# A hybrid encoder layer on one core: the end of the output projection, with halves split and part of the LayerNorm on TensorE

## The chip, the cores and the metric

The kernel runs on one core of one Trainium2 chip. The metric is the device time of one execution in microseconds (us). Each kernel also has one profiled execution, whose trace gives the start and length of every instruction; its time is counted from the trace's first to its last instruction (the span) and has a little around it.

The engines are named as in the profile: PE (TensorE, matrix products; PEld is its loading of weights), DVE (VectorE), ACT (ScalarE), POOL (GpSimd), SP (SyncE, which issues the DMAs here). "Granted clock" is the share of TensorE's full clock that the chip allowed at a moment.

## The reference

One layer works on 256 frames of width 4096. One input projection feeds sixteen heads of forgetting attention, 32 heads of an RWKV-7 recurrence and a gate. Their gated outputs `h` go through one output projection, and a LayerNorm closes the layer. What matters here is that end:

```python
h = jnp.concatenate([fox_out, rwkv_out], axis=-1) * jax.nn.silu(z.astype(f32))
out = jnp.einsum('bsc,cd->bsd', h.astype(x.dtype), w_out)
x = _layernorm(ALPHA * x.astype(f32) + out.astype(f32), ln_gain, ln_bias, LN_EPS)
```

where `_layernorm(x)` is `(x - mean) * rsqrt(var + eps) * gain + bias`, with mean and variance over the 4096 columns of a frame.

## The kernel before, in words

The 256 frames are two halves of 128 partitions, m = 0 and 1. The output projection runs over eight column blocks `b` of 512. In each block sixteen weight tiles `wo{b}_{q}` of 128 x 1024 come in from HBM (L651) and are split by `split` into a rounded high part on ACT (L135) and the rest on DVE (L136); each holds two k-slices of 128 rows. The pools behind the high and the low parts hold three tiles each. For each k-slice and each half there are three 512-column products (L663 to L665: high frames x high weights, low x high, high x low), which add up over 32 k-slices in one PSUM bank per half, `acc[m]`. The loop over m is the innermost, so both halves of a block end together.

After a block DVE forms ALPHA x + out in `res[m]` (L678) and its statistics (L679), and in all blocks but the last multiplies by the gain (L682). The residual, the gain and a five-row table `rows` of gain and bias were loaded and made block by block earlier (`load_tok`).

Behind the last block come the row factors, for both halves in one set of small instructions. They are: the statistics put together (L691), the square root on ACT (L692), the reciprocal `rs` (L694), minus mean times `rs` (L695) in a rounded and a rest part (L696 to L698, into `z5`), with the last block's gain products (L693, L699) between them. PE transposes `z5` into `zp` (L703), and ACT copies that into `l5` (L705), a 5 x 128 weight per half.

Then sixteen blocks are finished, half 0 first: a five-row product `l5` x `rows` into a PSUM tile `wp` (L711), and on DVE `res * rs + wp` (L712). Each pair of blocks is sent out by one DMA of 512 KB (L717); the last two blocks of half 1 go one by one (L714).

PSUM has eight banks in two pools. `pp` has two and `ps` six; a new tile of a pool waits until the tile that held its bank is done with. Within an engine instructions run in the order of the program's stream, which the framework's scheduler lays out when the program is built. A DMA waits in SP's queue in order.

Of the kernel before, what the change touches and what calls it, by code (L numbers as in the profile page):

```python
# [10 lines left out]
F32 = mybir.dt.float32  # L11
BF16 = mybir.dt.bfloat16
F32R = mybir.dt.float32r
AF = mybir.ActivationFunctionType
ALU = mybir.AluOpType
AX = mybir.AxisListType

P = 128
S = 256
D = 4096  # L20
KT = D // P
# [6 lines left out]
ALPHA = 2.0 ** 0.25  # L28
# [5 lines left out]
OB = 512  # L34
# [2 lines left out]
ROWS = 2  # L37
W = {"fr": 10, "fo": 3, "vs": 2, "np": 6, "gp": 5, "d1": 8, "d2": 8, "xp": 3, "fs": 4, "fp": 5}
NB = D // OB

PAR = ["w0", "a0", "k_k", "k_a", "r_k", "gn_gain", "gn_bias", "mu_r", "mu_k", "mu_v"]

# [35 lines left out]
def layer(ctx: ExitStack, tc: tile.TileContext, xt, xtok, w_lora, w_main, w_o, up, par, mulora, fbias, lng, lnb, cst, out, groups=G, dbg=None):  # L78
    nc = tc.nc
# [6 lines left out]
    pp = ctx.enter_context(tc.tile_pool(name="pp", bufs=2, space=PS))  # L86
    ps = ctx.enter_context(tc.tile_pool(name="ps", bufs=6, space=PS))
    def pst(name):
        return ps.tile([P, 512], F32, tag="ps", name=name)
# [35 lines left out]
    ident = cs[:, C_ID : C_ID + P]  # L125
# [6 lines left out]
    def split(src, n, name):  # L132
        hi = wpool.tile([P, 1024], F32R, tag="wh", name=name + "h")
        lo = wpool.tile([P, 1024], F32R, tag="wl", name=name + "l")
        nc.scalar.copy(hi[:, :n], src[:, :n])  # L135
        nc.vector.tensor_tensor(lo[:, :n], src[:, :n], hi[:, :n].bitcast(F32), ALU.subtract)  # L136
        return hi, lo
# [8 lines left out]
    for n, (k0, k1) in enumerate(pieces):  # L146
# [6 lines left out]
        hi, lo = split(l_raw[n], (k1 - k0) * LW, f"wl{n}")  # L153
        for k in range(k0, k1):
            o = (k - k0) * LW
            mm(acc_l[0], LORA + NF, hi, lo, o, k)
            mm(acc_l[1], LORA, hi, lo, o + LORA + NF, k)
        hi, lo = split(w_raw[n], (k1 - k0) * P, f"wr{n}")
# [35 lines left out]
    def slot():  # L194
        for g in list(sides):
            try:
                next(g)
            except StopIteration:
                sides.remove(g)
# [415 lines left out]
    ht = {}  # L615

    def get_h(k):
        while k not in hs:
            slot()
        t = xpool.tile([P, 2, S], F32R, tag=f"x{k}", name=f"h{k}")  # L620
        nc.scalar.copy(t[:, 0, :], hs[k])
        nc.vector.tensor_tensor(t[:, 1, :], hs[k], t[:, 0, :].bitcast(F32), ALU.subtract)
        ht[k] = t
# [6 lines left out]
    def load_tok(b):  # L630
        o = slice(b * OB, (b + 1) * OB)
        for m in range(2):
            nc.sync.dma_start(out=res[m][:, o], in_=xtok[m * P : (m + 1) * P, o])
        nc.sync.dma_start(out=lgain[:, o], in_=lng[:, o].to_broadcast([P, OB]))
        rr = rpool.tile([5, OB], F32, tag="rr", name=f"rr{b}")
        nc.sync.dma_start(out=rr[0:3], in_=lng[:, o].to_broadcast([3, OB]))
        nc.sync.dma_start(out=rr[3:5], in_=lnb[:, o].to_broadcast([2, OB]))
        rh = rpool.tile([5, OB], F32R, tag="rh", name=f"rh{b}")
        nc.scalar.copy(rh, rr)
        rt_ = rpool.tile([5, OB], F32, tag="rt", name=f"rt{b}")  # L640
        nc.vector.tensor_scalar(rt_, rh.bitcast(F32), cs[0:5, C_ROW : C_ROW + 1], None, ALU.mult)
        nc.vector.scalar_tensor_tensor(rows[:, o], rr, cs[0:5, C_ROW + 1 : C_ROW + 2], rt_, ALU.mult, ALU.add)

    res = None
    st = [const.tile([P, NB, 6], F32, name=f"lst{m}") for m in range(2)]
    for b in range(NB):
        pool, tag = (pp, "pp") if b % 2 == 0 else (ps, "ps")
        acc = [pool.tile([P, 512], F32, tag=tag, name=f"oacc{b}_{m}") for m in range(2)]
        for q in range(KT // 2):
            raw = wpool.tile([P, 1024], F32, tag="wr", name=f"wo{b}_{q}", bufs=4)  # L650
            nc.sync.dma_start(out=raw, in_=w_o[b][:, 2 * q : 2 * q + 2, :].rearrange("p k c -> p (k c)"))  # L651
            hi, lo = split(raw, 1024, f"wo{b}_{q}")
            for j in range(2):
                k = 2 * q + j
                if b == 0:
                    slot()
                    get_h(k)
                elif k == 4:
                    load_tok(b)
                o = slice(j * OB, (j + 1) * OB)  # L660
                for m in range(2):
                    tt = slice(m * P, (m + 1) * P)
                    nc.tensor.matmul(acc[m], ht[k][:, 0, tt], hi[:, o], start=(k == 0), stop=False)  # L663
                    nc.tensor.matmul(acc[m], ht[k][:, 1, tt], hi[:, o], start=False, stop=False)  # L664
                    nc.tensor.matmul(acc[m], ht[k][:, 0, tt], lo[:, o], start=False, stop=(k == KT - 1))  # L665
        if b == 0:
            assert not sides
            mid.close()
            rpool = ctx.enter_context(tc.tile_pool(name="rpool", bufs=1))
            res = [rpool.tile([P, D], F32, tag=f"res{m}", name=f"res{m}") for m in range(2)]  # L670
            lgain = rpool.tile([P, D], F32, name="lgain")
            rows = rpool.tile([5, D], F32R, name="rows")
            load_tok(0)
            lneps = const.tile([P, 1], F32, name="lneps")
            nc.vector.memset(lneps, LN_EPS)
        for m in range(2):
            o = slice(b * OB, (b + 1) * OB)
            nc.vector.scalar_tensor_tensor(res[m][:, o], res[m][:, o], ALPHA, acc[m], ALU.mult, ALU.add)  # L678
            nc.vector.bn_stats(st[m][:, b, :], res[m][:, o])  # L679
        if b < NB - 1:  # L680
            for m in range(2):
                nc.vector.tensor_tensor(res[m][:, o], res[m][:, o], lgain[:, o], ALU.mult)  # L682
    o = slice(D - OB, D)
    mv = rpool.tile([P, 2, 2], F32, name="mv")
    rs = rpool.tile([P, 2], F32, name="rs")
    s2 = rpool.tile([P, 2], F32, name="s2")
    zh = rpool.tile([P, 2], F32R, name="zh")
    z5 = rpool.tile([P, 2, 5], F32, name="z5")
    nc.vector.memset(z5, 1.0)
    for m in range(2):  # L690
        nc.vector.bn_aggr(mv[:, m, :], st[m].rearrange("p b s -> p (b s)"))  # L691
    nc.scalar.activation(rs, mv[:, :, 1], AF.Sqrt, bias=lneps)  # L692
    nc.vector.tensor_tensor(res[0][:, o], res[0][:, o], lgain[:, o], ALU.mult)  # L693
    nc.vector.reciprocal(rs, rs)  # L694
    nc.vector.scalar_tensor_tensor(s2, mv[:, :, 0], -1.0, rs, ALU.mult, ALU.mult)  # L695
    nc.vector.tensor_copy(zh, s2)  # L696
    nc.vector.tensor_copy(z5[:, :, 0:3:2], zh.bitcast(F32).unsqueeze(2).to_broadcast([P, 2, 2]))
    nc.vector.tensor_tensor(z5[:, :, 1], s2, zh.bitcast(F32), ALU.subtract)  # L698
    nc.vector.tensor_tensor(res[1][:, o], res[1][:, o], lgain[:, o], ALU.mult)  # L699
    l5 = []  # L700
    for m in range(2):
        zp = pst(f"zp{m}")
        nc.tensor.transpose(zp[:5, :P], z5[:, m, :], ident)  # L703
        t = rpool.tile([5, P], F32R, name=f"l5{m}")
        nc.scalar.copy(t, zp[:5, :P])  # L705
        l5.append(t)
    for m in range(2):
        for b in range(NB):
            o = slice(b * OB, (b + 1) * OB)
            wp = pp.tile([P, 512], F32, tag="pp", name=f"wp{m}_{b}") if b % 2 else pst(f"wp{m}_{b}")  # L710
            nc.tensor.matmul(wp, l5[m], rows[:, o], start=True, stop=True)  # L711
            nc.vector.scalar_tensor_tensor(res[m][:, o], res[m][:, o], rs[:, m : m + 1], wp, ALU.mult, ALU.add)  # L712
            if m == 1 and b >= NB - 2:
                nc.sync.dma_start(out=out[m * P : (m + 1) * P, o], in_=res[m][:, o])  # L714
            elif b % 2:
                o = slice((b - 1) * OB, (b + 1) * OB)
                nc.sync.dma_start(out=out[m * P : (m + 1) * P, o], in_=res[m][:, o])  # L717


def arrange(inputs):  # L720
# [10 lines left out]
    res["w_main"] = np.ascontiguousarray(np.stack([t.reshape(KT, P, G, P).transpose(2, 1, 0, 3) for t in (r, k, v, fq, fk, fv, zf, zr)], 1))  # L731
    wo = a["w_out"].reshape(2, G, P, NB, OB)
    res["w_o"] = np.ascontiguousarray(wo.transpose(3, 2, 1, 0, 4).reshape(NB, P, KT, OB))
# [27 lines left out]
```

## Time and profile before

| | |
|---|---|
| median of 3 runs | 2077.0 us (2075.1 to 2077.57) |
| profiled execution | 2079.26 us |
| its span | 2077.5 us |
| mean granted TensorE clock over the span | 0.993 |
| output written by the last nine DMAs | 4.19 MB |

Times in the rows below are microseconds from the span's start. A row of the timeline gives start, length, engine, line, operation, result<-operands, and how many instructions were merged into it, then the idle time before it and who ended it. A row of a table by stretches gives the stretch, its length, the busy time of each engine with its instructions (xN), then the granted clock, the share of the DMA engines in use and GB/s.

### The profile page before, as it was taken

Reading aid. Unit: us, or ns where it says so; the run is one execution under the profiler, and the core shown is the slowest. Engines: PE = TensorE matmul, PEld = TensorE weight load, DVE = VectorE, ACT = ScalarE, POOL = GpSimd, SP = SyncE. Lnnn points to the kernel's source line nnn. Section 1 sums busy time; section 2 is a strip of 40 time slices with the busy share of each in tenths; the row PEclk is TensorE's granted clock in tenths of the full one; section 3 lists DMA queues with packets and bytes.
Section 4 is the critical chain, followed back from the end, with each engine's and each line's share of the span. In section 5 each row is a group of like instructions: output and inputs, shape, how many; then the busy total and the mean of one; then the engine's idle time right before and its main releaser. Section 6 shows DMA issues by size and latency. Waiting matters only on the chain.

```text
span 2077.5 us, 32862 instructions
## 1 busy us (share of the span) xinstructions
PE 2030.4 (98%) x12430; PEld 1711.2 (82%) x12430; DVE 1482.1 (71%) x2919; ACT 1017.7 (49%) x1607; POOL 25.0 (1%) x138
## 2 busy tenths in 40 slices
PE   9999999999999999999999999999999999999997
PEld 7878888888888888888888888888887878888885
DVE  6867777777777767677777777777776786655555
ACT  6635454545454545454545454545453564433331
POOL 0000000000000000000000000000000000000000
PEclk9999999999999999999999999999999999999998
DMA  7545555555555555555555555555555557866664
GB/s 275 181 159 165 179 166 179 166 179 166 179 167 178 170 174 172 173 166 179 166 179 166 178 167 176 168 178 164 178 165 161 171 165 237 261 192 193 192 194 150
DMA packets 130862, 372.71 MB, mean 179 GB/s; under 512 B 31160, under 2 KB 40040, under 8 KB 130704
## 3 DMA queue, kind: packets, MB, share of 16 engines
q1 hardware_dynamic: 130704, 370.62, 56.0%
q8 instruction: 97, 1.59, 0.3%
q14 instruction: 61, 0.50, 0.1%
HBM read 364.23 MB, written 6.32 MB: 178 GB/s over the span
## 4 chain that ended last, share of the span: by engine, by line
PE 71%; DVE 17%; DMA 8%; issue 2%; SPq 1%; ACT 1%; DVEq 0%; ACTq 0%
PE acc L140 31%; PE acc L141 15%; PE oacc L663 6%; PE oacc L664 6%; PE oacc L665 6%; DVE xc L456 4%; DVE prod L455 3%; DVE w_1l L136 3%; DMA td<-xc 2%; DMA Nb<-nd 2%; DMA T<-td 2%; DMA nd<-gb 2%; DVE w_2l L136 2%; DVE w_3l L136 1%; DVE w_0l L136 1%
## 5 line engine op out<-in xcount | busy, mean ns | idle before, releaser
L140 PE MATMUL acc<-x,w_1h 128*128 128x512 f32 x1016 | 372.7, 403 | 0.4 <-ACT w_1h L135 0.4
L140 PE MATMUL acc<-x,w_2h 128*128 128x512 f32 x1016 | 372.6, 404 | 0.0
L140 PE MATMUL acc<-x,w_3h 128*128 128x512 f32 x1016 | 369.1, 401 | 0.0
L140 PE MATMUL acc<-x,w_0h 128*128 128x512 f32 x1016 | 369.1, 401 | 0.0
L141 PE MATMUL acc<-x,w_1l 128*128 128x256 f32 x1016 | 289.2, 285 | 23.5 <-DVE w_1l L136 23.5
L141 PE MATMUL acc<-x,w_2l 128*128 128x256 f32 x1016 | 284.9, 280 | 0.0
L141 PE MATMUL acc<-x,w_0l 128*128 128x256 f32 x1016 | 284.6, 280 | 0.0
L141 PE MATMUL acc<-x,w_3l 128*128 128x256 f32 x1016 | 284.3, 280 | 0.0
L140 PEld LDWEIGHTS acc<-x,w_1h 128*128 128x128 f32 x1016 | 191.7, 189 | 44.1 <-ACT w_1h L135 1.2
L140 PEld LDWEIGHTS acc<-x,w_0h 128*128 128x128 f32 x1016 | 190.6, 188 | 45.3
L140 PEld LDWEIGHTS acc<-x,w_3h 128*128 128x128 f32 x1016 | 190.5, 188 | 44.9
L140 PEld LDWEIGHTS acc<-x,w_2h 128*128 128x128 f32 x1016 | 191.5, 189 | 41.3
L141 PEld LDWEIGHTS acc<-x,w_1l 128*128 128x128 f32 x1016 | 192.9, 190 | 33.6 <-DVE w_1l L136 33.6
L135 ACT CAST w_2h<-w 128x1024 fp32r<-128x1024 f32 x127 | 133.2, 1049 | 133.7 <-PE acc L140 119.2
L135 ACT CAST w_0h<-w 128x1024 fp32r<-128x1024 f32 x127 | 133.2, 1049 | 126.6 <-PE acc L140 92.4
L141 PEld LDWEIGHTS acc<-x,w_2l 128*128 128x128 f32 x1016 | 192.3, 189 | 0.9 <-DVE w_2l L136 0.2
L141 PEld LDWEIGHTS acc<-x,w_3l 128*128 128x128 f32 x1016 | 191.8, 189 | 1.0 <-DVE w_3l L136 0.3
L141 PEld LDWEIGHTS acc<-x,w_0l 128*128 128x128 f32 x1016 | 191.9, 189 | 0.5 <-DVE w_0l L136 0.3
L136 DVE TENSOR_TENSOR w_0l<-w,w_0h 128x1024 fp32r<-128x1024 f32 x127 | 155.3, 1223 | 51.4 <-ACT w_0h L135 51.4
L135 ACT CAST w_1h<-w 128x1024 fp32r<-128x1024 f32 x127 | 132.8, 1046 | 105.2 <-PE acc L140 77.2
L136 DVE TENSOR_TENSOR w_2l<-w,w_2h 128x1024 fp32r<-128x1024 f32 x127 | 155.1, 1221 | 34.2 <-ACT w_2h L135 32.6
L136 DVE TENSOR_TENSOR w_1l<-w,w_1h 128x1024 fp32r<-128x1024 f32 x127 | 154.4, 1216 | 31.2 <-ACT w_1h L135 28.3
(691 smaller groups left out, 3228.5 us busy)
## 6 DMA issues: line engine op xcount, KB each, us to landing
w<-in_w_main_dram SPq DMA_DIRECT2D x508, 512.0 KB, 4.5
wo<-in_w_o_dram SPq DMA_DIRECT2D x128, 512.0 KB, 3.5
Nb<-nd SPq DMA_DIRECT2D x16, 512.0 KB, 5.0
res<-in_xtok_dram SPq DMA_DIRECT2D x16, 256.0 KB, 4.8
xr<-in_xt_dram SPq DMA_DIRECT2D x7, 512.0 KB
out_dram<-res SPq DMA_DIRECT2D x7, 512.0 KB, 2.7
lr<-in_w_lora_dram SPq DMA_DIRECT2D x7, 416.0 KB, 8.4
nb<-ncd SPq DMA_DIRECT2D x16, 128.0 KB, 4.7
```

The source lines that it names most:

```text
L135: nc.scalar.copy(hi[:, :n], src[:, :n])
L136: nc.vector.tensor_tensor(lo[:, :n], src[:, :n], hi[:, :n].bitcast(F32), ALU.subtract)
L140: nc.tensor.matmul(acc[:m, :], hi[:, o : o + m], xs[k].rearrange("p a t -> p (a t)"), start=(k == 0), stop=False)
L141: nc.tensor.matmul(acc[:m, :S], lo[:, o : o + m], xs[k][:, 0, :], start=False, stop=(k == KT - 1))
L455: nc.vector.tensor_tensor(prod[:, :, s + 1 :], nb[:, s : s + 1, s + 1 :].to_broadcast([P, NJ, w]), xc[:, :, s + 1 :], ALU.mult)
L456: nc.vector.tensor_reduce(xc[:, :, s : s + 1], prod[:, :, s:], AX.X, ALU.add)
L663: nc.tensor.matmul(acc[m], ht[k][:, 0, tt], hi[:, o], start=(k == 0), stop=False)
L664: nc.tensor.matmul(acc[m], ht[k][:, 1, tt], hi[:, o], start=False, stop=False)
L665: nc.tensor.matmul(acc[m], ht[k][:, 0, tt], lo[:, o], start=False, stop=(k == KT - 1))
```

## The change

The last three weight tiles (q = 13, 14, 15) of the last block are used half by half: half 1's eighteen products over them are put off until half 0's are all issued (`late`). The row factors are computed for each half by itself (`moments`, `row`), so that half 0's stand in the program ahead of half 1's end. The tile of ones under `z5` is set on POOL and no longer on DVE.

In three of the eight blocks of each half (1, 4 and 6) the finishing is done by PE and ACT: PE multiplies `res` by a 128 x 128 diagonal matrix `dg` of the row factors in 32-bit floating point, adds the five-row product into the same bank, and ACT copies the sum to `res`. The other five blocks are finished by DVE as before. `pp` holds the tiles of blocks 3 and 7, `ps` all others. `send` issues the same nine DMAs.

```diff
+LATE = 3
+BY_PE = (1, 4, 6)
...
                 for m in range(2):
-                    tt = slice(m * P, (m + 1) * P)
-                    nc.tensor.matmul(acc[m], ht[k][:, 0, tt], hi[:, o], start=(k == 0), stop=False)
-                    nc.tensor.matmul(acc[m], ht[k][:, 1, tt], hi[:, o], start=False, stop=False)
-                    nc.tensor.matmul(acc[m], ht[k][:, 0, tt], lo[:, o], start=False, stop=(k == KT - 1))
+                    if m and b == NB - 1 and q >= KT // 2 - LATE:
+                        late.append((k, j, hi, lo))
+                    else:
+                        project(acc[m], k, j, m, hi, lo)
...
+    def moments(m):
+        nc.vector.scalar_tensor_tensor(res[m][:, o], res[m][:, o], ALPHA, acc[m], ALU.mult, ALU.add)
+        nc.vector.bn_stats(st[m][:, NB - 1, :], res[m][:, o])
...
+        nc.gpsimd.memset(z5, 1.0)
+        nc.vector.bn_aggr(mv, st[m].rearrange("p b s -> p (b s)"))
+        nc.scalar.activation(rs, mv[:, 1:2], AF.Sqrt, bias=lneps)
+        nc.vector.tensor_tensor(res[m][:, o], res[m][:, o], lgain[:, o], ALU.mult)
+        nc.vector.reciprocal(rs, rs)
+        nc.vector.scalar_tensor_tensor(s2, mv[:, 0:1], -1.0, rs, ALU.mult, ALU.mult)
+        nc.vector.tensor_copy(zh, s2)
+        d = rpool.tile([P, P], F32, name=f"dg{m}")
+        nc.scalar.mul(d, ident, rs)
+        nc.vector.tensor_copy(z5[:, 0:3:2], zh.bitcast(F32).to_broadcast([P, 2]))
+        nc.vector.tensor_tensor(z5[:, 1:2], s2, zh.bitcast(F32), ALU.subtract)
...
+    def row(m, z5):
+        zp = pst(f"zp{m}")
+        nc.tensor.transpose(zp[:5, :P], z5, ident)
+        t = rpool.tile([5, P], F32R, name=f"l5{m}")
+        nc.scalar.copy(t, zp[:5, :P])
+        l5.append(t)
+
+    def finish(m, b):
+        o = slice(b * OB, (b + 1) * OB)
+        wp = pp.tile([P, 512], F32, tag="pp", name=f"wp{m}_{b}") if b % 4 == 3 else pst(f"wp{m}_{b}")
+        if b in BY_PE:
+            nc.tensor.matmul(wp, dg[m], res[m][:, o], start=True, stop=False)
+            nc.tensor.matmul(wp, l5[m], rows[:, o], start=False, stop=True)
+            nc.scalar.copy(res[m][:, o], wp)
+        else:
+            nc.tensor.matmul(wp, l5[m], rows[:, o], start=True, stop=True)
+            nc.vector.scalar_tensor_tensor(res[m][:, o], res[m][:, o], rss[m], wp, ALU.mult, ALU.add)
...
+    z0 = moments(0)
+    for k, j, hi, lo in late:
+        project(acc[1], k, j, 1, hi, lo)
+    row(0, z0)
+    finish(0, 0)
+    finish(0, 1)
+    z1 = moments(1)
+    send(0, 0, 2)
+    for b in range(2, NB):
+        if b == 4:
+            row(1, z1)
+        finish(0, b)
+        if b % 2:
+            send(0, b - 1, b + 1)
+    for b in range(NB):
+        finish(1, b)
+        if b >= NB - 2:
+            send(1, b, b + 1)
+        elif b % 2:
+            send(1, b - 1, b + 1)
```

In the built program PE's stream behind the last product of the projection is: transpose of half 0; half 0's blocks 0, 1 (diagonal and five-row product), 2, 3, 7; transpose of half 1; half 0's blocks 4 (both products), 5, 6 (both); half 1's blocks 0 to 7 in order. DVE's stream there is: half 1's residual sum; half 0's block 0; half 1's statistics; half 0's block 2; half 1's statistics put together, gain product and reciprocal; half 0's block 3; half 1's minus mean times `rs`; half 0's block 7; half 1's `zh` and `z5`; half 0's block 5; half 1's blocks 0, 2, 3, 5, 7.

More of the change, by code (lines that the diff above doesn't have):

```diff
@@ L642, in load_tok, with project @@
         nc.vector.scalar_tensor_tensor(rows[:, o], rr, cs[0:5, C_ROW + 1 : C_ROW + 2], rt_, ALU.mult, ALU.add)
+    def project(acc, k, j, m, hi, lo):
+        o = slice(j * OB, (j + 1) * OB)
+        tt = slice(m * P, (m + 1) * P)
+        nc.tensor.matmul(acc, ht[k][:, 0, tt], hi[:, o], start=(k == 0), stop=False)
+        nc.tensor.matmul(acc, ht[k][:, 1, tt], hi[:, o], start=False, stop=False)
+        nc.tensor.matmul(acc, ht[k][:, 0, tt], lo[:, o], start=False, stop=(k == KT - 1))
     res = None
+    late = []
     st = [const.tile([P, NB, 6], F32, name=f"lst{m}") for m in range(2)]
@@ L659, in layer @@
                     load_tok(b)
-                o = slice(j * OB, (j + 1) * OB)
                 for m in range(2):
-                    tt = slice(m * P, (m + 1) * P)
-                    nc.tensor.matmul(acc[m], ht[k][:, 0, tt], hi[:, o], start=(k == 0), stop=False)
-                    nc.tensor.matmul(acc[m], ht[k][:, 1, tt], hi[:, o], start=False, stop=False)
-                    nc.tensor.matmul(acc[m], ht[k][:, 0, tt], lo[:, o], start=False, stop=(k == KT - 1))
+                    if m and b == NB - 1 and q >= KT // 2 - LATE:
+                        late.append((k, j, hi, lo))
+                    else:
+                        project(acc[m], k, j, m, hi, lo)
         if b == 0:
@@ L675, in layer @@
             nc.vector.memset(lneps, LN_EPS)
-        for m in range(2):
+        if b < NB - 1:
             o = slice(b * OB, (b + 1) * OB)
-            nc.vector.scalar_tensor_tensor(res[m][:, o], res[m][:, o], ALPHA, acc[m], ALU.mult, ALU.add)
-            nc.vector.bn_stats(st[m][:, b, :], res[m][:, o])
-        if b < NB - 1:
+            for m in range(2):
+                nc.vector.scalar_tensor_tensor(res[m][:, o], res[m][:, o], ALPHA, acc[m], ALU.mult, ALU.add)
+                nc.vector.bn_stats(st[m][:, b, :], res[m][:, o])
             for m in range(2):
@@ L683, in layer @@
     o = slice(D - OB, D)
[L684 to L699, printed above, removed]
-    l5 = []
-    for m in range(2):
+    l5 = []
+    dg = []
+    rss = []
+    def moments(m):
+        nc.vector.scalar_tensor_tensor(res[m][:, o], res[m][:, o], ALPHA, acc[m], ALU.mult, ALU.add)
+        nc.vector.bn_stats(st[m][:, NB - 1, :], res[m][:, o])
+        mv = rpool.tile([P, 2], F32, name=f"mv{m}")
+        rs = rpool.tile([P, 1], F32, name=f"rs{m}")
+        s2 = rpool.tile([P, 1], F32, name=f"s2{m}")
+        zh = rpool.tile([P, 1], F32R, name=f"zh{m}")
+        z5 = rpool.tile([P, 5], F32, name=f"z5{m}")
+        nc.gpsimd.memset(z5, 1.0)
[9 more added lines that the diff above has]
+        nc.vector.tensor_tensor(z5[:, 1:2], s2, zh.bitcast(F32), ALU.subtract)
+        rss.append(rs)
+        dg.append(d)
+        return z5
@@ L702, in layer @@
+    def row(m, z5):
         zp = pst(f"zp{m}")
-        nc.tensor.transpose(zp[:5, :P], z5[:, m, :], ident)
+        nc.tensor.transpose(zp[:5, :P], z5, ident)
         t = rpool.tile([5, P], F32R, name=f"l5{m}")
@@ L706, in layer, with send @@
         l5.append(t)
[L707 to L717, printed above, removed]
+    def finish(m, b):
[6 more added lines that the diff above has]
+        else:
+            nc.tensor.matmul(wp, l5[m], rows[:, o], start=True, stop=True)
+            nc.vector.scalar_tensor_tensor(res[m][:, o], res[m][:, o], rss[m], wp, ALU.mult, ALU.add)
+    def send(m, b0, b1):
+        o = slice(b0 * OB, b1 * OB)
+        nc.sync.dma_start(out=out[m * P : (m + 1) * P, o], in_=res[m][:, o])
+    z0 = moments(0)
[18 more added lines that the diff above has]
+            send(1, b - 1, b + 1)
 def arrange(inputs):
```

## The prediction

> **What bounds the kernel now.** The page first. It shows that the change touches little of the whole.
>
> ```profile
> span 2077.5 us, 32862 instructions
> PEclk9999999999999999999999999999999999999998
> ```
>
> Only the last of 40 slices has a lower granted clock. All edits lie in the last 29 us, so I read the end of the chain of waits next.
>
> ```profile
> 2057.25 4.39 issue
> 2061.64 0.28 PE zp L703
> ...
> 2061.94 0.26 ACT l L705
> ...
> 2062.25 0.80 PE wp L711
> ...
> 2063.07 9.31 DVE res L712 x14
> ...
> 2073.04 0.66 DVE res L712
> ```
>
> The projection's products end at 2057.25. PE then stands still for 4.39 us, while the row factors are made. From 2063.07 DVE finishes a block every 0.66 us (9.31 / 14). Behind DVE stands the output; these rows are from SP's timeline, its waits, the DMA issues and the table by half microseconds:
>
> ```profile
> 2064.51 0.34 SPq L717 DMA_DIRECT2D out_dram<-res  x1
> 2073.07 1.00 SPq L714 DMA_DIRECT2D out_dram<-res  x2
> SPq L757 <- DMA out_dram<-res: 2.3, 1, 2.3
> out_dram<-res SPq DMA_DIRECT2D x7, 512.0 KB, 2.7
> 2065.00:2065.50 0.50, 0.50 (x2) 0.36 (x2) 0.50 (x2) 0.00 (x0) 0.00 (x0) 0.50 0.34 131
> 2075.50:2076.00 0.50, 0.00 (x0) 0.00 (x0) 0.00 (x0) 0.00 (x0) 0.00 (x0) 0.50 0.92 344
> ```
>
> The first DMA is issued at 2064.51 and its bytes flow from about 2065.3 (a third of its slice), 0.8 us later. They flow until just before 2076.0. The last issue ends at 2074.07 (2073.07 + 1.00), its landing is 2.3 us later, at 2076.4, and the span ends 1.1 us after that. So DVE and DMA bound the end together.
>
> The last view is a table by stretches, cut where the granted clock changes (next to last column). All its changes lie on one grid of 3.41 us.
>
> ```profile
> 10.77:14.19 3.42, 1.55 (x6) 0.94 (x7) 3.00 (x6) 2.76 (x8) 0.00 (x0) 1.00 1.01 366
> 14.19:17.60 3.41, 3.41 (x13) 2.60 (x12) 2.52 (x6) 1.79 (x5) 0.00 (x0) 0.50 1.04 414
> 123.42:126.83 3.41, 2.07 (x12) 1.51 (x10) 1.82 (x3) 2.87 (x5) 0.00 (x0) 1.00 0.63 191
> 1584.32:1587.73 3.41, 2.88 (x23) 2.25 (x23) 2.42 (x5) 1.43 (x3) 0.00 (x0) 0.50 0.46 142
> 2055.36:2058.78 3.42, 1.87 (x9) 1.21 (x7) 2.19 (x4) 0.00 (x0) 0.00 (x0) 1.00 0.00 0
> 2058.78:2062.19 3.41, 0.38 (x2) 0.12 (x2) 2.55 (x10) 0.54 (x3) 0.00 (x0) 1.00 0.00 0
> 2062.19:2065.60 3.41, 3.35 (x8) 2.34 (x9) 2.53 (x4) 0.16 (x2) 0.00 (x0) 0.50 0.08 32
> 2066.00:2070.00 4.00, 3.30 (x8) 1.78 (x6) 4.00 (x7) 0.00 (x0) 0.00 (x0) 0.50 1.00 396
> ```
>
> A stretch in which PE was busy 1.55 or 0.38 us was followed by half clock; after 1.87 or 2.07 us the clock stayed. At half clock a stretch full of 128-row products (3.41) brought the clock back, one with 2.88 did not, and neither did 3.35 us of the five-row products at 2062. So before, the whole finish ran at half clock, unnoticed, since DVE was slower. The last row also gives the output's rate: 396 GB/s, or 0.66 us for one 256 KB block.
>
> **The change part by part.** The times of the end come from the timeline:
>
> ```profile
> 2048.91 0.39 PE L663 MATMUL oacc<-wo_13h,h 128*128 128x512 f32 x1
> 2056.59 1.36 DVE L678 SCALAR_TENSOR_TENSOR res<-res,oacc 128x512 f32<-128x512 f32 x2 [5.40 <-PE oacc L665]
> 2056.84 0.39 PE L665 MATMUL oacc<-wo_15l,h 128*128 128x512 f32 x1
> 2057.87 1.28 DVE L679 BATCH_NORM_STATS2 lst<-res 128x6 f32<-128x512 f32 x2
> 2059.07 0.58 DVE L691 BATCH_NORM_AGGREGATE mv<-lst 128x2 f32<-128x48 f32 x2
> 2059.57 0.63 DVE L693 TENSOR_TENSOR res<-res,lgain 128x512 f32<-128x512 f32 x1
> 2059.69 0.29 ACT L692 ACTIVATE rs<-mv,lneps 128x2 f32<-128x2 f32 x1 [9.76 <-DVE mv L691]
> 2060.12 0.15 DVE L694 RECIPROCAL rs<-rs 128x2 f32<-128x2 f32 x1
> 2060.77 0.15 DVE L695 SCALAR_TENSOR_TENSOR s<-mv,rs 128x2 f32<-128x2 f32 x1
> ...
> 2061.16 0.17 DVE L697 COPY z<-zh 128x4 f32<-128x4 f32 x1
> 2061.24 0.16 DVE L698 TENSOR_TENSOR z<-s,zh 128x2 f32<-128x2 f32 x1
> 2061.60 0.12 PEld L703 LDWEIGHTS zp<-cs,z 128*5 128x5 f32 x2 [4.80 <-issue]
> ```
>
> *Products of the two halves apart.* The same 36 products, one every 0.227 us ((2056.84 - 2048.91) / 35). Half 0 ends eighteen of them, 4.08 us, ahead of PE's end at 2057.23, so at 2053.15. The three weight tiles held longer fill the pools' three buffers, but no later tile wants one. PE's end doesn't move.
>
> *Half 0's row factors.* One half costs 0.68 + 0.64 + 0.29 on DVE (half of the x2 rows), 0.29 on ACT, 0.15 for the reciprocal, and 0.83 from the next step to the transpose (2060.77 to 2061.60); with 0.05 to 0.1 for each hand-over about 3.2 us, to 2056.4. PE is busy until 2057.23: hidden, with 0.8 us over. The first block follows the transpose by 0.6 us (2061.64 to 2062.25), so at 2057.7. That takes 4.5 us off its 2062.25. The diagonal and the second square root lie on ACT, idle there; the two ones-tiles on POOL, long before; the sends' new waits for ACT stand in SP's queue, with nothing but later sends behind them.
>
> *The finish, prices.* These are the nearest rows for the new work: 32-bit products of 256 and 128 columns in two passes each, at half and at full clock; their weight load; and ACT's copy of a whole PSUM tile.
>
> ```profile
> 130.99 1.05 PE L580 MATMUL fop<-pT,vt 128*128 128x256 f32 x2
> 131.84 0.63 PE L581 MATMUL fop<-pT,vt 128*128 128x128 f32 x2
> ...
> 1694.74 0.59 PE L580 MATMUL fop<-pT,vt 128*128 128x256 f32 x2
> 1695.17 0.38 PE L581 MATMUL fop<-pT,vt 128*128 128x128 f32 x2
> ...
> L580 PEld LDWEIGHTS fop<-pT,vt x32: 187/188/333, 130.8 to 1694.7; 128*128 128x128 f32 x32
> ...
> L437 ACT COPY BKt<-tp 128x512 f32<-128x512 f32 x16 | 9.4, 587 | 0.2
> ```
>
> From start to start 256 columns took 0.43 us at full clock and 0.85 at half, so a 512-column diagonal product is 0.86 or 1.70. Bounds at half clock: 0.85, if its two passes went at the five-row products' rate (3.35 / 8 = 0.42), and 2.37, if its two loads of 0.333 stood open. I take 1.70, the same operation. ACT's six copies of 0.59 lie beside PE. Six of DVE's sixteen steps go (6 x 0.66 = 4.0 us).
>
> *Half 1's factors: the new wait.* At full clock PE runs block 0 at 2057.7, block 1 from 2057.9 (0.86 + 0.23; ACT has copied it by 2059.8, the first send), block 2 at 2059.0 and blocks 3 and 7, and is empty at 2059.8. In its stream the transpose of half 1 comes next, and everything else stands behind it. Half 1's factors can't be ready: DVE takes the residual sum to 2057.9, half 0's block 0 to 2058.75, statistics to 2059.4, half 0's block 2 to 2060.05, the rest up to the reciprocal to 2061.0, and then half 0's blocks 3 and 7 stand between, 1.3 us. `z5` is done at 2062.75 and the transpose starts at 2062.95. PE is idle for 3.1 us.
>
> *The clock.* If a 3.41 us stretch with 1.55 us of work or less halves the clock, nearly every position of the grid does so here: PE has about 2.4 us of work from 2057.2 to 2059.8, then none to 2062.95. Only stretches that begin within about half a microsecond of 2058.0 cut the hole so that both halves hold enough: 0.5 / 3.41, one in seven. The clock falls somewhere from 2061.7 to 2064.6.
>
> *Sum at half clock from 2062.95.* Left are five diagonal products (8.5 us) and eleven five-row ones (11 x 0.427 = 4.7, from the 1.70 / 4 of one such pass): 13.2 us, from 2063.05 to 2076.3. The last product is done 0.37 after its slot of 0.43 (0.80 in the chain), DVE needs 0.69, so the last block is ready at 2077.4, against 2073.70 before. The queue of DMAs, then long empty, needs from that issue 0.8 + 0.66 and 0.5 for the landing (2.7 less 0.8 and the 1.3 of 512 KB), where before it took 2.7 us with blocks still in line: 2079.4, and with the 1.1 at the end 2080.5. That is 3.0 us more. Where the clock falls later than 2063.05, up to 1.6 us of the work goes at full rate; over the grid's positions that saves 0.4 on average. I take +2.6.
>
> The profiled execution's 2079.26 (span and 1.8 us around it) would become 2081.9; the three runs lie 2.3 lower at 2077.0, so on their scale 2079.6.
>
> **The rivals.**
>
> *The clock stays full.* The hole of 3.1 us is shorter than a stretch. Then from 2063.0 on: the fourth and fifth blocks of half 0 are sent at 2065.2 (0.86 + 0.23 + 0.39 to the five-row product's end, DVE 0.69), and the twelve blocks then left need 12 x 0.66 = 7.9 us of output, from 2066.0 to 2073.9, against 2076.0: -2.1, 2074.9. Against it: the row with 1.55 us of work, 45% busy. [...] The trace here halves it already after stretches that were not empty.
>
> *The clock comes back after one stretch.* PE is then fully busy, as in 14.19:17.60. From about 2066.5 at full rate PE is done by 2071.7, and the output bounds: sent from 2066.7, 2067.5 + 7.9 = 2075.4, -0.6: 2076.4. Against it: the 3.35 us of five-row products brought nothing back, and they are a third of this mix (0.85 of 2.56 us); a stretch with 2.88 didn't either.
>
> *Slower: the diagonal's weight loads stand open.* Each is two passes with a load of 0.333 us at half clock. In full, 5 x 2 x 0.333 = 3.3 more: 2082.9. Past 0.16 us a load ((4.2 - 2.6) / 10) it exceeds 0.2%. Against it: 0.85 us from start to start leaves no room between passes of 256 columns.
>
> *It doesn't do what it says.* If half 0's transpose waited for both halves' factors, as before, at 2062.95 at the earliest, 5.9 us behind PE's end, half 0's five blocks would follow it too: at half clock 5 x 0.43 + 1.70 = 3.8 us more, 2083.4. The built stream speaks against it: half 0's `z5` stands ahead of all of half 1's work on DVE.
>
> **How the numbers follow.** The forecast, half clock to the end, has 0.58, back after one stretch 0.17, full 0.13, open loads 0.09, others 0.03. About 0.2% (4.2 us) is what a measurement of this kernel can tell from no change: 2072.8 to 2081.2. The forecast's own range is 2078.4 (the latest fall, 1.6 saved) to 2081.2 (an output end of 3.8 us as before, transpose 0.5 later); with a fifth of its chance above, slower gets 0.12 + 0.09 + 0.02. Faster needs less than 2072.8: output at its rate from 2066.0 forbids it even at full clock, so 0.04 for runs that scatter (2075.1 to 2077.57). The range holds from the full-clock case, also that of diagonal products at the lower bound, to the forecast's upper end.
>
> **What would show it.** Right: half 0's first block near 2057.7 and the first send near 2059.8; PE idle for about 3 us ahead of half 1's transpose; granted clock 0.50 in the last 12 us; diagonal products 1.70 apart; a last DVE step near 2077 with the DMA engines partly idle from 2062 on. Wrong: clock 1.00 behind that hole, no hole, or ACT or the output as the last bound.

## The result and the profile after

The changed kernel took 2084.17 us (median of 7 runs, 2079.76 to 2089.28) against 2077.0 us (7 runs, 2073.47 to 2077.62): a ratio of 1.0034, 95% interval 1.0021 to 1.0048. It is slower by about 7 us, where +2.6 us had been forecast, in a range from 2074.9 (full clock) to 2081.2.

The page of the kernel after hides this. Its span is only 1.5 us longer than the 2077.5 before:

```profile
span 2079.0 us, 32905 instructions
```

The time up to the end of the output projection differs from one execution to the next. One example is the clock in the middle of the two profiled executions. Here are ten microseconds of each around the same step of the attention heads, from the table by stretches; behind the five engines' busy times stands the granted clock. First before, then after:

```profile
1582.00:1592.00 10.00, 8.14 (x42) 6.37 (x43) 6.33 (x12) 3.03 (x5) 0.00 (x0) 0.66 0.47 147
```

```profile
1577.00:1587.00 10.00, 7.78 (x56) 6.03 (x55) 6.98 (x15) 4.13 (x7) 0.00 (x0) 1.00 0.47 149
```

Before, that stretch was granted 0.66 of the clock, after, all of it. In all, the projection ended at 2057.25 in the one and at 2052.09 in the other, 5.2 us apart, though up to there the edits give PE the same work, in another order. So I compare the *tail*: from the end of the projection's last product to the end of the span. It was 20.2 us before (2077.5 - 2057.25) and is 26.9 us after (2079.0 - 2052.09): +6.7 us, in keeping with the runs. Each tail below is worked out in the same way.

The chain of waits of the kernel after shows where it goes:

```profile
2051.86 0.23 PE oacc L651
2052.09 0.12 PE zp L722
...
2052.54 0.49 PE wp L735
2053.03 1.06 PE wp L731 x2
2054.08 0.43 PE wp L732
...
2058.34 0.37 PE zp L722
2058.72 1.71 PE wp L731 x2
...
2061.57 2.01 PE wp L731 x2
2063.58 0.72 PE wp L732
2064.30 0.43 PE wp L735
...
2074.65 0.75 DVE res L736
```

L731 is the diagonal product, L732 the five-row product added to it, L735 the five-row product of a DVE block, L722 the transpose. Half 0's first block starts 0.45 us behind the projection, as planned. Half 1's transpose (2058.34) is 6.25 us behind it. From there to its last product PE is the chain, in a pattern of 2.01 + 0.72 + 0.43 = 3.16 us (the first diagonal product alone took 1.71). The table by stretches of the same kernel has the clock:

```profile
2052.00:2055.20 3.20, 2.86 (x9) 1.14 (x7) 2.45 (x4) 0.84 (x2) 0.00 (x0) 1.00 0.00 0
2055.20:2058.00 2.80, 0.02 (x1) 0.00 (x0) 2.70 (x9) 0.69 (x2) 0.00 (x0) 1.00 0.50 199
2058.00:2062.00 4.00, 3.66 (x6) 1.53 (x7) 0.59 (x3) 0.84 (x2) 0.00 (x0) 0.50 0.31 123
2062.00:2066.00 4.00, 4.00 (x6) 1.00 (x4) 1.11 (x2) 0.58 (x1) 0.00 (x0) 0.50 0.39 156
```

PE is empty from 2055.2, the clock is halved at 2058.0 and stays so with PE fully busy. DVE (0.59 and 1.11 of 4 us) and the DMA engines (0.31 and 0.39) now wait for PE. The waits say the same:

```profile
DVE res L736 <- PE wp L735: 13.4, 7, 3.4
PEld wp L732 <- issue: 8.3, 6, 1.5
...
PE zp L722 <- DVE z L715: 3.1, 1, 3.1
...
PEld wp L731 <- issue: 2.2, 4, 0.7
```

The third line is the *hole*, PE's idle time ahead of half 1's transpose. The second and the last are new: the weight loads of the five-row products behind a diagonal product, and those of the diagonal products, begin late, though nothing that the profile shows holds them. Such a load *stands open*: the one of the five-row product behind the first diagonal product of half 1 starts at 2060.35 (0.28 us), together with its product, and PE waits for it; that of the next five-row product (0.33) starts at 2060.52, 0.43 us ahead of its product at 2060.95, and is hidden behind the running one.

### The profile page after: what moved, and what is told of

The parts are those of the page before. It is cut to its first block, busy times and chain, and to the rows that moved or that the text cites. A ratio compares the mean times of both kernels' runs of the same rounds, so it can differ in the third digit from the quotient of the medians.

```text
span 2079.0 us, 32905 instructions
## 1 busy us (share of the span) xinstructions
PE 2037.8 (98%) x12442; PEld 1710.7 (82%) x12442; DVE 1479.4 (71%) x2917; ACT 1023.0 (49%) x1616; POOL 27.8 (1%) x140
## 4 chain that ended last, share of the span: by engine, by line
PE 74%; DVE 15%; DMA 7%; issue 2%; SPq 1%; ACT 1%; DVEq 0%; ACTq 0%
PE acc L142 33%; PE acc L143 16%; PE oacc L650 6%; PE oacc L649 6%; PE oacc L651 6%; DVE xc L458 3%; DVE prod L457 3%; DVE w_1l L138 2%; DMA td<-xc 2%; DMA Nb<-nd 2%; DMA nd<-gb 1%; DMA T<-td 1%; DVE w_2l L138 1%; DVE w_0l L138 1%; DVE w_3l L138 1%
```

## The experiments

| kernel | projection ends | span | tail | ratio to before, interval |
|---|---|---|---|---|
| before | 2057.2 | 2077.5 | 20.2 | |
| after | 2052.1 | 2079.0 | 26.9 | 1.0034 (1.0021 to 1.0048) |
| after, once more | 2049.7 | 2076.6 | 26.9 | 1.0016 (1.0002 to 1.0030) |
| no diagonal products | 2054.8 | 2074.1 | 19.2 | 0.9994 (0.9984 to 1.0004) |
| rows padded to 128 | 2057.1 | 2078.5 | 21.4 | 1.0011 (0.9995 to 1.0026) |
| products in the hole | 2058.6 | 2078.4 | 19.7 | 0.9993 (0.9981 to 1.0005) |
| both cures | 2059.7 | 2078.1 | 18.4 | 1.0000 (0.9986 to 1.0013) |
| nothing postponed | 2050.3 | 2080.5 | 30.2 | 1.0044 (1.0027 to 1.0061) |
| before, rows padded | 2049.0 | 2069.3 | 20.3 | 1.0009 (0.9993 to 1.0025) |
| reordered | 2053.3 | 2069.7 | 16.5 | 0.9989 (0.9977 to 1.0002) |
| reordered, once more | 2055.2 | 2071.7 | 16.5 | 0.9977 (0.9965 to 0.9990) |
| reordered, no diagonal products | 2055.2 | 2073.6 | 18.4 | 0.9988 (0.9971 to 1.0004) |

The ends of the projection scatter over 10.7 us, so most intervals of the ratio can't part these kernels. The tails can: each of the two kernels that were run twice has the same tail in both executions, to 0.1 us. The kernel before was profiled once; with padded rows, and the same work in its tail, it has 20.3.

**No diagonal products.** The other edits stay.

```diff
-BY_PE = (1, 4, 6)
+BY_PE = ()
```

> No diagonal products: all sixteen blocks are finished by five-row products and DVE; the halves' ends and row factors stay apart. 'Tail' is the time from the end of the projection's last product to the end of the span: 20.2 us before, 26.9 us after the change. Theory (the diagonal products at half clock make the loss, 2.01 + 0.72 + 0.43 us a block pair instead of 1.70 + 0.43 + 0.43): DVE bounds, sixteen steps of 0.66 us plus 3 us for half 1's own factors, tail 17 to 18, about 2.5 us faster than before. Rival (the splitting of the halves, with its hole of 3.1 us ahead of half 1's transpose, makes the loss): tail 20 or more.

Tail 19.2: below the rival's 20, above my 17 to 18. Splitting the halves does gain, 1.0 us; the six diagonal products, as they stand in the changed kernel, cost 7.7. The missing 1.2 us is in DVE's timeline:

```profile
2060.01 0.74 DVE L736 SCALAR_TENSOR_TENSOR res<-res,rs,wp 128x512 f32<-128x512 f32 x1
...
2060.99 0.15 DVE L715 TENSOR_TENSOR z<-s,zh 128x1 f32<-128x1 f32 x1
2062.42 7.33 DVE L736 SCALAR_TENSOR_TENSOR res<-res,rs,wp 128x512 f32<-128x512 f32 x11 [1.28 <-PE wp L735]
```

Half 0's later blocks stand behind half 1's transpose in PE's stream, so DVE idles 1.28 us until it is through.

**Rows padded to 128.** The five-row weight and table get 123 rows of zeros; sums and products are unchanged.

```diff
+        nc.gpsimd.memset(rows[:, o].bitcast(F32), 0.0)
...
-        rows = rpool.tile([5, D], F32R, name="rows")
+        rows = rpool.tile([P, D], F32R, name="rows")
...
+    l5z = [rpool.tile([P, P], F32R, name=f"l5{m}") for m in range(2)]
+    for m in range(2):
+        nc.gpsimd.memset(l5z[m].bitcast(F32), 0.0)
...
-        t = rpool.tile([5, P], F32R, name=f"l5{m}")
-        nc.scalar.copy(t, zp[:5, :P])
+        t = l5z[m]
+        nc.scalar.copy(t[0:5, :], zp[:5, :P])
```

> The changed kernel with the five-row products padded by zeros to 128 rows; the same sums, no new product. Theory (five-row products count for nothing with the clock gate, and weight loads stand open only where a product of few rows meets one of 128): the clock comes back one stretch of 3.4 us after PE is busy again, and a diagonal product at half clock takes 1.70 and its five-row successor 0.43; tail 20 to 22. Without the return but with hidden loads: tail 24. Rival (32-bit weight loads always stand open and the clock stays down whatever the rows): tail 26.9 as after the change.

Tail 21.4, as the theory has it. Its chain of waits (here L735 is the diagonal product, L736 and L739 the two others), and its clock by stretches of 3.41 us:

```profile
2063.00 0.37 PE zp L726
2063.37 1.71 PE wp L735 x2
2065.08 0.43 PE wp L736
2065.51 0.43 PE wp L739
...
2068.49 1.07 PE wp L735 x2
2069.56 0.23 PE wp L736
```

```profile
2061.96:2065.37 3.41, 2.37 (x5) 1.27 (x6) 0.79 (x4) 0.25 (x1) 0.00 (x0) 0.50 0.39 154
2065.37:2068.79 3.42, 3.42 (x7) 1.93 (x6) 1.01 (x2) 1.17 (x2) 0.00 (x0) 0.50 0.35 143
```

The hole and the fall of the clock are still there, but the pattern at half clock is 1.71 + 0.43 + 0.43, the prediction's own price, and not 3.16. And the clock is back at 2068.79, in the middle of a diagonal product (1.07). It was at half for two stretches, but PE, which started again at 2063.00, was busy for only 2.37 us of the first; the first full one brought the clock back, as the theory had it. Both effects come from the rows alone, as 32-bit and rounded products alternate here just the same.

**Products in the hole.** Thirteen 128-row products that nobody reads, ahead of half 1's transpose.

```diff
+            wd = pst("wd")
+            for n in range(13):
+                nc.tensor.matmul(wd, ht[0][:, 0, :P], late[-1][2][:, :512], start=True, stop=True)
             row(1, z1)
```

> The changed kernel with thirteen 128-row products that nobody reads on PE in the hole ahead of half 1's transpose. Theory (the hole halves the clock): granted clock 1.00 well past the transpose, a diagonal product about 1.06 and the rest at full rate, tail 18 to 20. Rival (the cost of the diagonal products doesn't hang on the clock, they just stand one behind the other with open loads): tail 25 to 27.

Tail 19.7. Chain of waits and table by stretches:

```profile
2061.54 3.17 PE wd L754 x13
2064.71 0.11 PE zp L722
2064.82 0.86 PE wp L731 x2
2065.68 0.42 PE wp L732
2066.10 0.23 PE wp L735
2066.32 1.06 PE wp L731 x2
```

```profile
2065.00:2070.00 5.00, 5.00 (x14) 1.83 (x12) 2.15 (x3) 1.49 (x4) 0.00 (x0) 1.00 0.48 191
```

The clock stays whole, and 7.2 us of the tail are gone with no edit to the work itself. The open loads remain, at full clock 0.2 + 0.2 us a diagonal product (1.06 against 0.86, 0.42 against 0.23); only the first, behind the 128-row transpose, has its load hidden. In this kernel the scheduler also moved one block of half 0 behind half 1's transpose, which came 6.07 us behind the projection instead of 6.25. So 0.2 us of the gain need not be the clock's; from the transpose to its last product PE took 8.95 us (2064.71 to 2073.66) instead of 16.3.

**Both cures.** Padded rows and products in the hole together.

> The changed kernel with both cures: rows padded to 128 and thirteen unread products in the hole. Theory: clock 1.00 to the end, 1.29 us for a diagonal product and its two followers (0.86 + 0.23 + 0.23) against 1.70 with open loads at full clock, tail 18 to 19, bound by the output behind half 1's transpose. Rival (loads at full clock cost nothing): as with the products in the hole alone, 19.7.

Tail 18.4, and in its chain of waits every diagonal product is as expected:

```profile
2065.28 0.86 PE wp L735 x2
2066.14 0.23 PE wp L736
2066.36 0.23 PE wp L739
```

**Nothing postponed.**

```diff
-LATE = 3
+LATE = 0
```

> The changed kernel without the postponed products: both halves end together, separate factors and the diagonal products stay. Theory: PE is idle for 4.5 us, so all six diagonal products run at half clock, sixteen five-row products as well: 6 x 2.6 + 10 x 0.43 = 20 us from 5 us behind the projection, tail 28 to 30. Rival (the early start of half 0 gains nothing, as the end is bound elsewhere): tail 26.9 as after the change.

Tail 30.2, just beyond the 28 to 30 expected. Postponing eighteen products is worth 3.3 us in the changed kernel. In its chain of waits PE is idle for 4.18 us, nearly as before, and the first diagonal product is already at half clock:

```profile
2050.34 4.18 issue
...
2056.03 2.00 PE wp L731 x2
```

**Before, rows padded.** The padding alone, on the kernel before.

> The kernel before with its five-row products padded to 128 rows. Theory (DVE and output bound there, the half clock went unnoticed): the clock comes back during the finish, tail 20.2 as before. Rival (PE's half clock did cost time before): tail 18 to 19.

Tail 20.3. In the table by stretches the clock comes back in the finish, and DVE is still busy all the time: the half clock had cost the kernel before nothing.

```profile
2055.00:2059.00 4.00, 4.00 (x10) 2.81 (x10) 4.00 (x7) 0.00 (x0) 0.00 (x0) 0.50 0.44 176
...
2060.00:2063.00 3.00, 1.00 (x2) 0.37 (x2) 3.00 (x6) 0.00 (x0) 0.00 (x0) 0.97 1.00 397
```

**Reordered.** On the padded kernel: half 1's factors ahead of half 0's finish in the program, half 0's transpose ahead of the last three postponed products, and the diagonal products where PE would wait (blocks 1 to 3 of half 0; 2 and 5 of half 1).

```diff
-BY_PE = (1, 4, 6)
+BY_PE = ((1, 2, 3), (2, 5))
...
     z0 = moments(0)
-    for k, j, hi, lo in late:
+    for k, j, hi, lo in late[:-1]:
         project(acc[1], k, j, 1, hi, lo)
     row(0, z0)
-    finish(0, 0)
-    finish(0, 1)
+    k, j, hi, lo = late[-1]
+    project(acc[1], k, j, 1, hi, lo)
     z1 = moments(1)
-    send(0, 0, 2)
-    for b in range(2, NB):
-        if b == 4:
-            row(1, z1)
+    for b in range(4):
+        finish(0, b)
+        if b % 2:
+            send(0, b - 1, b + 1)
+    row(1, z1)
+    for b in range(4, NB):
         finish(0, b)
```

> The split halves, five-row products padded to 128 rows, half 1's factors on DVE ahead of all but one of half 0's blocks, and the diagonal products where PE would wait: blocks 1, 2 and 3 of half 0, blocks 2 and 5 of half 1. Theory (the hole and the open loads made the loss, not the diagonal products as such): no hole over 1 us, granted clock 1.00 until half 1's blocks, the output nearly unbroken from 3 us behind the projection (10.5 us of bytes and 1.6 behind them), tail 15 to 16.5, 4 us faster than before. Rival (a diagonal product on PE and ACT can't pay): tail no better than the 19.2 us of the kernel without them.

Tail 16.5. Half 0's transpose, 0.26 us of PE, now lies ahead of the projection's end, so against the kernels without this order the tail reads about 0.3 us too short. The chain of waits and the DMA engines' busy tenths in 40 slices of its last 17.7 us:

```profile
2053.26 0.23 PE wp L739
2053.49 0.86 PE wp L735 x2
2054.35 0.23 PE wp L736
...
2056.76 0.25 PE wp L739
...
2057.03 5.36 DVE res L740 x8
...
2063.05 0.66 DVE res L740
```

```profile
DMA  0000000009980199739999999999999999910000
```

The diagonal products fill what was the hole, at 0.86 us and full clock, and the output, broken twice near its beginning, is the bound. So the diagonal product itself does pay where PE has its full clock and would wait. The same without any diagonal product:

> The same without any diagonal product. Theory: DVE bounds (sixteen steps of 0.66 and 3 us of half 1's factors), the clock may fall but five-row products stay under DVE's pace; tail 17.5 to 19. Rival (the diagonal products bring nothing where DVE and output bound): tail as in the kernel with them.

Tail 18.4: they are worth 1.9 us here. Both kernels were then run once more:

> The changed kernel once more. Theory: the tail hangs on the hole and the mixed rows, not on where the grid of the clock happens to lie: a hole of 3.1 us, half clock from it to the end, 3.15 us for a diagonal product and its two followers, tail 25 to 27. Rival (the profiled execution fell badly on the grid): clock 1.00 behind the hole, tail 18 to 20.

> The version with reordered factors, padded rows and the diagonal products in the wait, once more. Theory: tail 16 to 17, the time about 3.7 us below the kernel before. Rival (one lucky profile): tail 18 or more.

The changed kernel's tail is again 26.9, the reordered one's again 16.5, now with a ratio of 0.9977 (0.9965 to 0.9990): about 0.2% faster than the kernel before, where the first interval (0.9977 to 1.0002) had left it open. The changed kernel's second ratio, 1.0016, is 3.3 us (0.4 to 6.2) and so close to the forecast. In its profiled execution the tail is again 6.7 us longer, so I put that closeness down to the scatter ahead of the tail; the other executions have no trace. In the second execution of the changed kernel the clock fell at another place in the hole, 3.6 us behind the projection (0.67 of a microsecond's clock) and not 5.9, with no effect on the tail, since PE is idle there. The first row is the whole stretch of 3.41 us ahead of that fall:

```profile
2049.93:2053.34 3.41, 2.68 (x7) 1.14 (x7) 2.79 (x5) 0.77 (x2) 0.00 (x0) 1.00 0.00 0
...
2053.00:2054.00 1.00, 0.00 (x0) 0.00 (x0) 1.00 (x5) 0.29 (x1) 0.00 (x0) 0.67 0.40 160
```

PE was busy for 2.68 us of it, more than in the prediction's rows after which the clock stayed (1.87 and 2.07); but 1.62 of the 2.68 were five-row products and only 1.06 a diagonal one.

## Why the prediction was wrong

The mechanism was the one forecast: a hole, half clock behind it, PE as the last bound. What failed is a term of its sum, the price of the diagonal products at half clock, which was too small; two smaller terms were short as well.

- *Half 0's early start* came as worked out: factors done 0.9 us ahead of PE's end, first block at +0.45 us (0.5 predicted).
- *The hole* was 3.1 us, as predicted. Half 1's transpose came 6.25 us behind the projection instead of 5.7: at full clock too the diagonal product of block 1 has open loads (1.06 + 0.43 against 0.86 + 0.23), so DVE had block 2 later and stood idle for 0.37 us ahead of it.
- *The clock* fell in the hole and stayed at half to the end, so the rivals of a full clock and of a return after one stretch fell. It fell 5.9 us behind the projection in one execution and 3.6 in the other, where the prediction's rule of busy time had 4.5 to 7.4 (2061.7 to 2064.6). By that rule the stretch with 2.68 us should have kept the clock: here the rule failed, without a cost. PE had been idle for 2.8 us at the one fall and for 0.5 at the other. The whole hole was 3.1 us, shorter than a stretch of 3.41, and the clock fell in it all the same.
- *The price of a diagonal product* failed. "I take 1.70, the same operation" is right for 128 rows next to 128 rows, from which the row came (and in the padded kernel, 1.71). Next to five-row products it is 2.01, and its follower 0.72 instead of 0.43: 0.59 to 0.60 more each (the first, behind the transpose, only 0.29). From the transpose to the end of PE's last product it took 16.3 us (2058.34 to 2074.65) instead of 13.7: 2.6 us too little in the sum, the largest error. The rival "weight loads stand open" had this in kind, at 0.67 a product, with 9 in 100, and was argued down with a row in which no product of few rows had a part.
- *The end of the output* took 3.6 us behind the last DVE step (2075.40 to 2079.0), 0.5 more than predicted. The sum had the queue "long empty"; but the block before the last was sent only 0.6 us ahead of it (2074.83 and 2075.42), so the last bytes flowed until 2077.2, 1.8 us behind the DVE step instead of the 1.5 of the sum. That is 0.3 of the 0.5; the rest was not followed.

These three terms, 0.5 + 2.6 + 0.5, make up 3.6 of the 3.7 us between +3.0 in the sum and the tail's +6.7. The forecast of +2.6 had taken off another 0.4 for a later fall of the clock, of which the two executions show nothing: it fell ahead of the transpose in both.

## What to carry to other kernels

Price an operation by a row that has the same neighbours, not only the same shape: a weight load hidden in one stream can stand open in another (here 0.43 us a five-row product against 0.72). Before PE is given work to take it off another engine, look at the granted clock where that work will stand, and at what PE waits for just ahead of it. And where the body of a kernel scatters from run to run, compare the changed stretch by itself, from one fixed event to the end.

## What the runs showed of the hardware

- Weight loads were hidden behind the running product where both products had the same number of rows (128 next to 128, in the padded kernel: 1.71 and 0.43 us at half clock; five next to five, in the kernel before: 0.42, 3.35 us for eight). They stood open at each change between five and 128: 0.3 us into the diagonal product (2.01) and 0.3 out of it (0.72) at half clock, 0.2 each at full (1.06 against 0.86, 0.42 against 0.23). Why they did, no run here shows.
- Five-row products did not bring the clock back. In the kernel before they kept PE busy for 3.35 of the 3.41 us from 2062.19 at 0.50, and the clock stayed there. Mixed with diagonal products, in the kernel after, they kept 0.50 for about 16 us, through three stretches that PE filled (3.42, 3.41 and 3.41 us from 2061.41 on). The same stream padded with rows of zeros was back 5.8 us after PE started again, with its first full stretch. The zeros change no sum; what about the added rows brought the clock back was not tried.
- Busy time alone didn't tell when the clock fell. In the changed kernel a stretch with 2.68 us, mostly five-row products, was followed by half clock in the second execution, and one with 1.89 us, sixteen of its 23 products of 32 rows, in the first (126.06 to 129.47); in the kernel before one with 1.87 us of nine 128-row products (2055.36 to 2058.78) was not.
